# A two-layer diffusion step: first modulation by matrix products, HGRN level updates in one instruction, row broadcasts from two rounded parts

## The chip, the cores and the metric

The kernel runs on one core of one Trainium2 chip. The metric is the device time of one execution in microseconds (us). The kernel before takes 2850.07 us (median of three runs, 2849.15 to 2854.26). Everything below is told from one execution that the hardware profiler recorded. The engines are PE (TensorE, with its weight loads as PEld), DVE (VectorE), ACT (ScalarE), POOL (GpSimd) and SP (SyncE, which issues most DMAs).

## What is computed

One denoising step of a trunk with two layers, on 512 latent tokens and 128 prompt tokens of 1024 features, all in fp32. Cut to what matters here:

```python
def _modulation(cvec, w, b):                                  # once for c, once for c_ctx
    return (silu(cvec) @ w + b).reshape(cvec.shape[0], 9, D_MODEL)
def _ffn_sublayer(x, mod, j, g, b, w1, w3, w2):
    shift, scale, gate = _mod_parts(mod, j)
    h = x * (1 + scale) + shift
    y = (silu(h @ w1) * (h @ w3)) @ w2
    return _layernorm(ALPHA * x + 0.5 * gate * y, g, b)
for l in range(DEPTH):                # ffn, mixer, ffn; each with shift, scale, gate of its own
    ...
    # mixer of l = 0: windowed attention and a two-way mLSTM; l = 1: attention and a two-way HGRN2:
    #   S_t = diag(f_t) S_{t-1} + k_t v_t^T,  k_t = 1 - f_t,  o_t = S_t^T q_t
```

## The kernel before

Activations lie transposed: eight tiles of 128 features (`k`, KD = 8) by 640 tokens, handled in two halves of 384 and 256 tokens (HALVES; the prompt is the last 128). A product in nearly full precision is made of three products of rounded parts (`mm3`): the operand is split into a rounded part, copied by ACT (line 123), and the rest, subtracted by DVE (line 126). Weights come through four raw buffers (`rawp`, tag raw) and are split into `wp` (tile `w`) or `vp` (tile `wv`). The tokens `rawx` have buffers of their own.

A Python program writes the instructions in order and a scheduler puts each engine's queue in order, so every engine runs a fixed list. SP's list issues the loads, and a load whose buffer is still in use holds up all that stand behind it on SP.

`start` (lines 268 to 323) makes shift and scale of the first sublayer from two 1024x1024 blocks of `ada_w`. For each of eight column blocks `m` it loads two 1024x128 pieces (one DMA each), multiplies rows by silu(c) and adds them up on DVE (tile `acc`, lines 130 and 133), ACT (`acp`) and POOL (line 308), and lets PE add over the partitions by products with a vector of ones (`pm<-ones,acc`). After a block's shift and scale `mod`, `spread` makes the modulated tile `h` on ACT and splits it. The modulations of all later sublayers are a filler (`ada`, line 334, 128x512 steps on DVE), spread over the feed-forward layers.

`norm` (line 390) makes 1/sigma on POOL (`rs`), then broadcasts the rows rs and -mean*rs over the partitions by fp32 products with the identity (`prs`, `pnm`). The mLSTM of the even mixer broadcasts two rows for each head and direction in the same manner (`nmu`, line 1056, and `ab`, line 1073). They come from `ma`.

`hgrn_head` (line 1280) computes the decayed products of a head with a tree of seven levels. Tiles Q and K hold both directions (K = 1 - f, on POOL, line 1288). In levels 0 to 4, ACT gathers half of K of each direction into `kc` (two instructions), PE makes twenty 32x32 products (`lv`), and DVE puts the wanted ones into `diag` (line 1314). Then four updates of 128x320 elements multiply a half of each of Q and K by the level's totals, two on DVE and two on POOL (lines 1337 and 1338), and two small products make the totals of the next level (`hi<-hi`). Heads 0 and 1 run beside the projections of later heads (`weave`, temporaries `xarena` and `hw`), heads 2 and 3 with nothing but each other (`harena`).

Of the kernel before, what the change touches and what calls it, by code (L numbers as in the profile page):

```python
# [49 lines left out]
class Net:  # L50
# [146 lines left out]
    def setup(self):  # L197
# [30 lines left out]
        for row in rows:  # L228
            if row is None:
                pos = -(-pos // P) * P  # L230
                continue
# [11 lines left out]
    def vectors(self, b):  # L243
# [24 lines left out]
    def start(self, out):  # L268

        nc = self.nc  # L270
        w = self.i["ada_w"][0]
# [4 lines left out]
        sc = self.sc.rearrange("p (c k) -> p k c", c=2)
        most, dve = KD - 1, 1

        def finish(m, raw, acc):

            ps = self.pm()
            for part in range(2):
                o = ps[:, 2 * part:2 * part + 2]
                for k in range(most, KD):
                    self.mm(o, raw[:, part, k], sc[:, k], k == most, False)
                for n, t in enumerate(acc):
                    c = min(n, 1)
                    self.mm(o[:, c:c + 1], t[:, part * P:(part + 1) * P], self.ones, False, n == 2)
            for part in range(2):
                self.act(out[:, part, :, m], ps[:, 2 * part:2 * part + 2], AF.Identity, bias=b1[:, part, m:m + 1])  # L290
            a, b = HALVES[0]
            self.spread(0, m, self.x[:, m, a:b], out[:, 1], out[:, 0])
# [1198 lines left out]
```

## Time and profile before

| | |
|---|---|
| median of 3 runs | 2850.07 us |
| profiled execution, its own time | 2846.81 us |
| its span | 2845.0 us |
| PE busy | 2703.4 us, 95% |
| DVE busy | 1819.8 us, 64% |
| ACT, POOL busy | 961.4 us, 353.8 us |

The stages, by the timeline: first feed-forward layer to about 550 us, even mixer to 936, feed-forward to 1415, feed-forward of layer 1 to 1855, odd mixer to 2366 (HGRN heads from about 2140 to 2283), last feed-forward layer to the end. PE's busy time is modelled by the profiler, so 95% is no statement on its peak. Idle time of an engine counts only where the next stage waits for it.

### The profile page before, as it was taken

To read this page: it belongs to the slowest core of one execution; us is meant where nothing else is said; L and a number is where in the kernel's file an instruction comes from. 1 tells how busy PE (TensorE), PEld (TensorE's weight loads), DVE (VectorE), ACT (ScalarE), POOL (GpSimd) and SP (SyncE) were. 2 spreads that over 40 slices of the span, in tenths; PEclk is the share of its full clock that TensorE was granted. 3 is DMA by queue.
4 is the path that set the end of the run, shared out by engine and by line. 5 is a ranking of instruction groups with operands and counts; after the bars stand their busy time and mean duration, and the time that the engine had idled before them with its cause. 6 is when DMAs were issued, how large, how long until landed. Compare 5 with 4: busy or idle time off the path is not lost.

```text
span 2845.0 us, 47283 instructions
## 1 busy us (share of the span) xinstructions
PE 2703.4 (95%) x19221; PEld 2597.6 (91%) x19221; DVE 1819.8 (64%) x3573; ACT 961.4 (34%) x2009; POOL 353.8 (12%) x394
## 2 busy tenths in 40 slices
PE   6999999989998999999999999999998689999998
PEld 6999999988887999999899999988788589999997
DVE  8876765777657976533796773475677769333335
ACT  5411211555544421311432122155553435112122
POOL 4000000411003100000400000041104522000003
PEclk9999999999999999999999999999999799999999
DMA  7554543121222544422264452130111224223110
GB/s 197 177 149 126 168 122 102 61 63 39 63 69 70 151 146 126 126 67 75 60 181 132 124 165 82 45 97 20 42 42 51 75 71 132 71 73 97 60 53 38
DMA packets 321526, 270.56 MB, mean 95 GB/s; under 512 B 13834, under 2 KB 273692, under 8 KB 321308
## 3 DMA queue, kind: packets, MB, share of 16 engines
q1 hardware_dynamic: 320948, 267.39, 32.1%
q8 instruction: 151, 2.47, 0.4%
q14 instruction: 67, 0.55, 0.1%
q10 hardware_dynamic: 360, 0.14, 0.0%
HBM read 258.31 MB, written 9.18 MB: 94 GB/s over the span
## 4 chain that ended last, share of the span: by engine, by line
PE 73%; DVE 13%; DMA 5%; ACT 3%; issue 3%; POOL 2%; SPq 0%; DVEq 0%; ACTq 0%; POOLq 0%
PE ps L136 35%; PE po L136 21%; PE pj L136 5%; PE pn L136 3%; DVE acc L133 3%; DMA rawa<-in_ada_w 2%; DMA raw<-in_ffn_w 2%; PE pv L136 2%; DVE w L126 2%; PE pT L139 1%; PE s L136 1%; DVE wv L126 1%; DVE x L133 1%; DVE h L126 1%; DVE sum L126 1%
## 5 line engine op out<-in xcount | busy, mean ns | idle before, releaser
L136 PE MATMUL ps<-h,w 128*128 128x256 f32 (+1 forms) x7584 | 1122.9, 309 | 2.1 <-DVE h L126 1.8
L136 PEld LDWEIGHTS ps<-h,w 128*128 128x128 f32 x7584 | 1116.2, 190 | 3.5 <-DVE h L126 2.4
L136 PE MATMUL po<-g,wv 128*128 128x256 f32 (+1 forms) x4224 | 631.6, 310 | 6.7 <-DVE x L133 6.4
L136 PEld LDWEIGHTS po<-g,wv 128*128 128x128 f32 x4224 | 621.3, 188 | 14.1 <-DVE x L133 8.7
L133 DVE SCALAR_TENSOR_TENSOR x<-po,mod,x 128x128 f32<-128x128 f32 (+1 forms) x576 | 235.6, 435 | 277.2 <-PE po L136 275.8
L133 DVE SCALAR_TENSOR_TENSOR acc<-rawa,sc,acc 128x512 f32<-128x512 f32 (+1 forms) x496 | 351.2, 747 | 12.9 <-DMA rawa<-in_ada_w 11.5
L126 DVE TENSOR_TENSOR w<-raw,w 128x1024 fp32r<-128x1024 f32 x212 | 261.0, 1236 | 132.4 <-ACT w L123 131.8
L123 ACT ACTIVATE wv<-raw 128x1024 fp32r<-128x1024 f32 x116 | 120.1, 1055 | 568.3 <-PE po L136 451.4
L123 ACT ACTIVATE w<-raw 128x1024 fp32r<-128x1024 f32 x212 | 222.6, 1056 | 168.2 <-issue 76.7
L463 POOL TENSOR_TENSOR ssq<-ssq,sq 128x384 f32<-128x384 f32 (+1 forms) x84 | 84.1, 1001 | 1340.3 <-ACT sq L123 1318.8
L123 ACT ACTIVATE g<-gt 128x384 fp32r<-128x384 f32 (+1 forms) x176 | 82.1, 467 | 405.9 <-DVE gt L126 405.9
L126 DVE TENSOR_TENSOR wv<-raw,wv 128x1024 fp32r<-128x1024 f32 x116 | 143.0, 1239 | 95.4 <-ACT wv L123 95.1
L126 DVE TENSOR_TENSOR gt<-sl,ps 128x384 f32<-128x384 f32 (+1 forms) x176 | 85.4, 485 | 182.6 <-PE ps L136 177.6
L136 PE MATMUL pj<-h,w 128*128 128x256 f32 (+1 forms) x1056 | 185.2, 318 | 0.9 <-ACT w L123 0.8
L136 PEld LDWEIGHTS pj<-h,w 128*128 128x128 f32 x1056 | 161.4, 192 | 8.0 <-issue 3.4
L123 ACT ACTIVATE sl<-ps 128x384 f32<-128x384 f32 (+1 forms) x176 | 75.9, 433 | 224.9 <-PE ps L136 224.7
L136 PE MATMUL ps<-h,wv 128*128 128x256 f32 (+1 forms) x864 | 138.4, 312 | 2.9 <-ACT h L123 1.5
L136 PE MATMUL pn<-w,h 128*128 128x256 f32 x960 | 137.6, 289 | 0.0
L136 PEld LDWEIGHTS ps<-h,wv 128*128 128x128 f32 x864 | 127.5, 190 | 5.3 <-DVE h L126 2.1
L136 PEld LDWEIGHTS pn<-w,h 128*128 128x128 f32 x960 | 126.0, 193 | 1.2
L126 DVE TENSOR_TENSOR g<-gt,g 128x384 fp32r<-128x384 f32 (+1 forms) x176 | 85.7, 487 | 27.3 <-ACT g L123 27.3
L424 POOL TENSOR_SCALAR x<-x,agb 128x384 f32<-128x384 f32 (+1 forms) x80 | 74.0, 927 | 103.2 <-ACT h L123 71.9
(345 smaller groups left out, 2672.1 us busy)
## 6 DMA issues: line engine op xcount, KB each, us to landing
raw<-in_ffn_w SPq DMA_DIRECT2D x264, 512.0 KB, 3.9
rawa<-in_ada_w SPq DMA_DIRECT2D x144, 512.0 KB, 3.8
raw<-in_w_in_odd SPq DMA_DIRECT2D x18, 512.0 KB, 3.9
raw<-in_w_in_even SPq DMA_DIRECT2D x14, 512.0 KB, 4.0
raw<-in_w_in_even SPq DMA_DIRECT2D x16, 256.0 KB, 3.5
raw<-in_w_out_even SPq DMA_DIRECT2D x8, 512.0 KB, 4.6
raw<-in_w_in_odd SPq DMA_DIRECT2D x16, 256.0 KB, 3.3
raw<-in_w_out_odd SPq DMA_DIRECT2D x8, 512.0 KB, 4.5
```

The lines of the kernel that those rows point to most:

```text
L123: return self.nc.scalar.activation(out=out, in_=in_, func=func, **k)
L126: return self.nc.vector.tensor_tensor(out=out, in0=in0, in1=in1, op=op)
L133: return self.nc.vector.scalar_tensor_tensor(out=out, in0=in0, scalar=s, in1=in1, op0=op0, op1=op1)
L136: return self.nc.tensor.matmul(out=out, lhsT=lhsT, rhs=rhs, start=start, stop=stop)
L139: self.nc.tensor.transpose(out, in_, self.ident[:in_.shape[0], :in_.shape[0]])
L424: nc.gpsimd.tensor_scalar(out=x, in0=x, scalar1=agb[:, 0, k:k + 1], scalar2=agb[:, 1, k:k + 1], op0=ALU.mult, op1=ALU.add)
L463: nc.gpsimd.tensor_tensor(out=sums[1], in0=sums[1], in1=sq, op=ALU.add)
```

## The change

The first modulation: `ada_w` is loaded by rows, two contiguous 128x1024 pieces for each of eight `k`. PE multiplies them by silu(c), as a stationary operand of 32 columns of which two are used, in fp32, with four 512-column results in four column groups of the array. ACT and DVE copy the results to SBUF, and sixteen small products (`adat`) add up the groups and turn the rows into columns. Of the tokens, tile 0 is loaded before the last row block and the others after it. The weights of the first feed-forward block are asked for behind the first `h`.

The norms and the mLSTM broadcast rows that were split into two rounded parts (`spread_rows`: two products with a rounded identity in place of one fp32 product). The mLSTM's scratch moves from the pool `yp` to `fp`, with buffers of its own for the gate weights' staging.

The HGRN levels: K and Q of both directions lie in one tile of four planes, so one ACT instruction gathers `kc`, one DVE instruction of 1280 elements updates what a level changes, and one product makes the totals. 1 - f is made on ACT. The diff, cut to its core:

```diff
+    def spread_rows(self, out, cols):
+        for n, c in enumerate(cols):
+            self.mm(out, c.to_broadcast([P, out.shape[0]]), self.identr, n == 0, n == 1)
...
+        self.identr = c.tile([P, P], F32R, name="identr")
+        self.act(self.identr, self.ident)
...
+        z = self.ft(KD * 32, "scz").rearrange("p (k c) -> p k c", k=KD)
+        nc.gpsimd.memset(z, 0.0)
+        nc.vector.tensor_copy(out=z[:, :, 0:2], in_=self.sc.rearrange("p (c k) -> p k c", c=2))
...
-        late = None
-        for m in range(KD):
-            raw = self.vt((2, KD, P), F32, "rawa")
-            acc = [self.ft(2 * P, "acc") for _ in range(3)]
-            for part in range(2):
-                c0 = part * D + m * P
-                nc.sync.dma_start(out=raw[:, part], in_=w[:, c0:c0 + P].rearrange("(k p) c -> p k c", p=P))
-            av = [t.rearrange("p (a b) -> p a b", a=2) for t in acc]
-            for k in range(most):
-                self.ada_step(av[:2] if k < dve else av[:1], raw[:, :, k], k)
-            for k in range(dve, most):
-                t = av[2] if k == dve else self.ft(2 * P, "acp").rearrange("p (a b) -> p a b", a=2)
-                self.act(t, raw[:, :, k], scale=self.sc[:, 8 + k:9 + k])
-                if k > dve:
-                    nc.gpsimd.tensor_tensor(out=av[2], in0=av[2], in1=t, op=ALU.add)
-            if m == 0:
-                self.load_x(0)
-            if late is not None:
-                finish(*late)
-            late = m, raw, acc
-        finish(*late)
+        acc = [self.bank(t, "ada") for t in ("a1", "a2", "b", "b")]
...
+        for k in range(KD):
+            raw = self.vt((2048,), F32, "rawa")
+            for n in range(2):
+                c = slice(1024 * n, 1024 * n + 1024)
+                nc.sync.dma_start(out=raw[:, c], in_=w[k * P:(k + 1) * P, c])
+            if k == KD - 2:
+                self.load_x(0, (0,))
+            for q in range(4):
+                g = (k + q) % 4
+                self.mm(acc[q][32 * g:32 * g + 32], z[:, k], raw[:, 512 * q:512 * q + 512], k < 4, k >= 4)
+        rows = self.vt((4, 512), F32, "rows")
+        ps = self.pm("adat")
+        for q in (2, 0, 3, 1):
+            if q < 2:
+                nc.vector.tensor_copy(out=rows[:, q], in_=acc[q])
+            else:
+                self.act(rows[:, q], acc[q])
+        for q in (2, 0, 3, 1):
+            for m in range(4):
+                o = 2 * (4 * q + m)
+                self.mm(ps[:, o:o + 2], rows[:, q, m * P:(m + 1) * P], self.fold[:, 0:2])
+        pv = ps[:, 0:4 * KD].rearrange("p (a m c) -> p a c m", a=2, c=2)
+        for part in (1, 0):
+            self.tt(out[:, part], pv[:, part], b1[:, part, None, :].to_broadcast([P, 2, KD]), ALU.add)
+        self.load_x(0, (1, 2))
...
+                self.first = self.ffn_units(0, 0, 0, False)
         yield 1
-        self.load_x(1)
...
-        rs = self.sm(4, "rs")
+        rn = self.sm(8, "rn")
+        rs, nm = rn[:, 0:4], rn[:, 4:8]
         nc.gpsimd.tensor_tensor(out=rs[:, :nch], in0=var[:, :nch], in1=self.mhalf[:, :nch], op=ALU.pow)
-        nm = self.sm(4, "nmr")
         self.stt(nm[:, :nch], mean, -1.0, rs[:, :nch], ALU.mult, ALU.mult)
+        rn = rn.rearrange("p (a b) -> p a b", a=2)[:, :, :nch]
+        hl = self.small.tile([P, 2, 2, 4], F32R, tag="rnp", name="rnp")
+        hl = hl[:, 0, :, :nch], hl[:, 1, :, :nch]
+        self.split(*hl, rn)
         pr, pn = self.pm("prs"), self.pm("pnm")
-        for t, o in ((rs, pr), (nm, pn)):
+        for t, o in enumerate((pr, pn)):
             for c in range(nch):
-                self.mm(o[:, c * P:(c + 1) * P], t[:, c:c + 1].to_broadcast([P, P]), self.ident)
+                self.spread_rows(o[:, c * P:(c + 1) * P], [v[:, t, c:c + 1] for v in hl])
...
-        mc = Arena(self.yp.tile([P, self.YN], F32, tag="y", name="mc"))
+        mc = Arena(self.fp.tile([P, self.FN], F32, tag="f", name="mc"))
...
+        pair = self.pair("ma")
+        tmp = Arena(self.ft(384, "mtmp"))
...
+        self.act(pair[0], ma, scale=sgn)
+        self.stt(pair[1], ma, sgn, pair[0].bitcast(F32), ALU.mult, ALU.subtract)
...
-                self.mm(nmu[:, :b - a], nident[:, r:r + 1].to_broadcast([64, P]), ma[0:64, a:b])
+                for q in range(2):
+                    self.mm(nmu[:, :b - a], self.identr[0:64, r:r + 1].to_broadcast([64, P]), ma[q][0:64, a:b], q == 0, q == 1)
...
-                self.mm(ab[:, :b - a], self.ident[64:128, 64 + r:64 + r + 1].to_broadcast([64, P]), ma[64:128, a:b])
+                for q in range(2):
+                    self.mm(ab[:, :b - a], self.identr[64:128, 64 + r:64 + r + 1].to_broadcast([64, P]),
+                            ma[q][64:128, a:b], q == 0, q == 1)
...
-        Q, K = (t.rearrange("p (d t) -> p d t", d=2) for t in temps[0:2])
-        S, kcs = qT, temps[2:4]
-        for pl in (1, 0):
-            nc.gpsimd.tensor_scalar(out=K[:, pl], in0=ft[pl], scalar1=-1.0, scalar2=1.0, op0=ALU.mult, op1=ALU.add)
-            self.tt(Q[:, pl], qT, ft[pl], ALU.mult)
+        qk = temps[0].rearrange("p (d t) -> p d t", d=4)
+        base = qk[:, 0, 0:1]
+        Q, K = (qk[:, 1], qk[:, 2]), (qk[:, 3], qk[:, 0])
+        S, kcs = qT, temps[1:3]
+        ff = ft.rearrange("p d t -> p (d t)")
+        view = lambda t, off, *ap: bass.AP(tensor=t.tensor, offset=t.offset + off, ap=[t.ap[0]] + [list(a) for a in ap])
+        self.act(qk[:, 0::3], ft, AF.Identity, scale=-1.0, bias=1.0)
+        self.tt(view(base, 2 * NT, (-NT, 2), (1, NT)), ft, qT[:, None, :].to_broadcast([P, 2, NT]), ALU.mult)
...
-                self.act(halves(kc)[:, :, 0], halves(K[:, 1])[:, :, 0])
-                self.act(halves(kc)[:, :, 1], halves(K[:, 0])[:, :, 1])
-                qb = Q[:, 0, 0:1]
+                self.act(kc.rearrange("p (n two h) -> p n two h", two=2, h=hh),
+                         view(base, 0, (2 * hh, nb), (3 * NT + hh, 2), (1, hh)))
...
-            tot = [t.rearrange("p (n two) -> p n two", two=2) for t in tb]
-            br = lambda t: t[:, :, None].to_broadcast([P, nb, hh])
-            q0, k0, q1, k1 = halves(Q[:, 0]), halves(K[:, 0]), halves(Q[:, 1]), halves(K[:, 1])
-            self.tt(q1[:, :, 1], q1[:, :, 1], br(tot[1][:, :, 0]), ALU.mult)
-            self.tt(k1[:, :, 0], k1[:, :, 0], br(tot[1][:, :, 1]), ALU.mult)
-            nc.gpsimd.tensor_tensor(out=q0[:, :, 0], in0=q0[:, :, 0], in1=br(tot[0][:, :, 1]), op=ALU.mult)
-            nc.gpsimd.tensor_tensor(out=k0[:, :, 1], in0=k0[:, :, 1], in1=br(tot[0][:, :, 0]), op=ALU.mult)
-            tb = []
-            for d in range(2):
-                dst = ft[d][:, :nb]
-                self.tt(dst, tot[d][:, :, 0], tot[d][:, :, 1], ALU.mult)
-                tb.append(dst)
+            x = view(base, 0, (2 * hh, 2 * nb), (2 * NT + hh, 2), (1, hh))
+            one = ff[:, 0:1]
+            self.tt(x, x, view(one, 1, (2, 2 * nb), (-1, 2), (0, hh)), ALU.mult)
+            tot = ff[:, :4 * nb].rearrange("p (n two) -> p n two", two=2)
+            self.tt(ff[:, :2 * nb], tot[:, :, 0], tot[:, :, 1], ALU.mult)
```

Three places in the order of the instructions. The first is SP's list at the start of the program, before:

```order
L201 DMA ident<-in_c_ident 128x128
L300 DMA rawa<-in_ada_w 128x8x128 x2
L258 DMA rawx<-in_x_sample 128x1024 x3
L300 DMA rawa<-in_ada_w 128x8x128 x14
L163 DMA raw<-in_ffn_w 128x8x128 x4
L346 DMA rawa<-in_ada_w 128x2x512 x2
L163 DMA raw<-in_ffn_w 128x8x128 x2
L258 DMA rawx<-in_x_sample 128x1024
L258 DMA rawx<-in_x_prompt 128x1024
```

and now:

```order
L206 DMA ident<-in_c_ident 128x128
L299 DMA rawa<-in_ada_w 128x1024 x14
L271 DMA rawx<-in_x_sample 128x1024
L299 DMA rawa<-in_ada_w 128x1024 x2
L271 DMA rawx<-in_x_sample 128x1024 x2
L168 DMA raw<-in_ffn_w 128x8x128 x4
L356 DMA rawa<-in_ada_w 128x2x512 x2
L168 DMA raw<-in_ffn_w 128x8x128 x2
L168 DMA raw<-in_ffn_w 128x1024
L271 DMA rawx<-in_x_sample 128x1024
L271 DMA rawx<-in_x_prompt 128x1024
```

The loads of `ada_w` were sixteen column pieces behind three token tiles; now they are sixteen row pieces, with one token tile ahead of the last two and two behind. The second half's tokens stand behind one more weight load.

The second place is DVE's list in the HGRN levels of heads 2 and 3 (`harena` holds Q and K, `hi` the totals, `lv` and `diag` the 32x32 products), before:

```order
L126 TENSOR_TENSOR hi_20894<-hi_20894 128x160 x2
L1314 COPY_PREDICATED diag_22337<-lmask_21225,lv_22422 128x160
L126 TENSOR_TENSOR harena_22273<-harena_22273,hi_21357 128x160x2 x2
L126 TENSOR_TENSOR hi_20895<-hi_20895 128x160
L126 TENSOR_TENSOR hi_21357<-hi_21357 128x160
L1314 COPY_PREDICATED diag_22279<-lmask_21225,lv_22452 128x160
L126 TENSOR_TENSOR harena_22273<-harena_22273,hi_20894 128x80x4 x2
L126 TENSOR_TENSOR hi_20894<-hi_20894 128x80 x2
L1314 COPY_PREDICATED diag_22337<-lmask_21225,lv_22482 128x160
```

and now:

```order
L126 TENSOR_TENSOR harena_22057<-harena_22057,hi_20748 128x320x2x2
L1346 COPY_PREDICATED diag_22112<-lmask_21079,lv_22186 128x160
L126 TENSOR_TENSOR hi_20748<-hi_20748 128x320
L126 TENSOR_TENSOR harena_22057<-harena_22057,hi_20749 128x320x2x2
L1346 COPY_PREDICATED diag_22061<-lmask_21079,lv_22211 128x160
L126 TENSOR_TENSOR hi_20749<-hi_20749 128x320
```

For a level and head, two updates of 320 elements and two products of totals became one update of 1280 elements and one product. POOL's two updates have left its list.

The third is PE's list ahead of the even mixer (`po` is the last product of the feed-forward layer's second half, `wg` the gate weights of the mLSTM, `wv` those of a projection), before:

```order
L136 MATMUL pj_5286<-h_98,wg_5240 128x384 x6
L136 MATMUL pj_5398<-h_98,wv_5273 128x384 x3
L136 MATMUL po_5048<-g_4505,wv_4510 128x256
L136 MATMUL po_5069<-g_4505,wv_4510 128x256
L136 MATMUL pj_5398<-h_98,wv_5273 128x384 x3
L136 MATMUL pj_5286<-h_98,wg_5240 128x384
L136 MATMUL po_5048<-g_4505,wv_4510 128x256 x2
L136 MATMUL po_5048<-g_4506,wv_4515 128x256 x3
```

and now, in two pieces, first the start of `po`:

```order
L136 MATMUL po_4817<-g_4266,wv_4271 128x256
L136 MATMUL po_4838<-g_4266,wv_4271 128x256
L136 MATMUL po_4817<-g_4266,wv_4271 128x256 x2
L136 MATMUL po_4817<-g_4267,wv_4276 128x256 x3
L136 MATMUL po_4817<-g_4268,wv_4281 128x256 x3
```

then what follows the last `po`, at the second half's norm:

```order
L136 MATMUL prs_5000<-identr_107,rnp_4997 128x128 x4
L136 MATMUL pnm_5001<-identr_107,rnp_4997 128x128 x4
L136 MATMUL pj_5065<-h_98,wg_5017 128x384 x24
L136 MATMUL pj_5119<-h_98,wv_5047 128x384 x6
L136 MATMUL pj_5177<-h_98,wv_5052 128x384 x24
```

The products with `wg`, which stood between those of `po`, now stand behind the norm's broadcasts.

## Rows read from the trace of the kernel before

**Rows 1.** The page, busy time of each engine over the span.

```profile
PE 2703.4 (95%) x19221; PEld 2597.6 (91%) x19221; DVE 1819.8 (64%) x3573; ACT 961.4 (34%) x2009; POOL 353.8 (12%) x394
```

**Rows 2.** Windows: stage, busy us of each engine, granted clock, DMA share, GB/s.

```profile
0.00:85.00 85.00, 57.06 (x277) 52.89 (x278) 68.31 (x121) 45.72 (x111) 38.42 (x51) 1.00 0.72 194
85.00:545.00 460.00, 457.00 (x3128) 453.68 (x3127) 330.75 (x556) 121.90 (x191) 21.92 (x27) 1.00 0.44 131
...
760.00:860.00 100.00, 94.64 (x610) 79.56 (x609) 58.72 (x219) 45.73 (x157) 4.84 (x7) 1.00 0.25 63
...
2225.00:2280.00 55.00, 31.70 (x746) 27.05 (x745) 46.22 (x94) 18.92 (x47) 33.14 (x33) 0.72 0.09 30
```

**Rows 3.** Windows inside the start, same columns.

```profile
30.00:38.00 8.00, 5.01 (x24) 4.84 (x23) 7.86 (x12) 5.93 (x16) 6.87 (x9) 1.00 1.16 283
75.00:76.00 1.00, 0.51 (x5) 0.54 (x6) 0.00 (x0) 0.00 (x0) 0.00 (x0) 1.00 1.06 430
```

**Rows 4.** Groups of instructions, 0 to 85 us: count, busy, mean ns, idle before.

```profile
L308 POOL TENSOR_TENSOR acc<-acc,acp 128x256 f32<-128x256 f32 x40 | 32.9, 825 | 27.7 <-ACT acp L123 23.3 <-DVE acc L133 1.8
L133 DVE SCALAR_TENSOR_TENSOR acc<-rawa,sc,acc 128x256 f32<-128x256 f32 x48 | 32.8, 684 | 1.0
L136 PE MATMUL pm<-ones,acc 128*128 128x1 f32 x96 | 21.7, 340 | 11.8 <-DVE acc L133 8.5 <-POOL acc L308 3.3
...
L264 DVE COPY x<-pm 128x512 f32<-128x512 f32 x10 | 6.7, 685 | 3.8 <-PE pm L139 3.8
...
L123 ACT ACTIVATE h<-x,mod 128x384 f32<-128x384 f32 x8 | 5.6, 704 | 0.1
...
L123 ACT ACTIVATE w<-raw 128x1024 fp32r<-128x1024 f32 x4 | 4.2, 1055 | 0.0
L123 ACT ACTIVATE h<-h 128x384 fp32r<-128x384 f32 x8 | 4.1, 511 | 0.0
...
L123 ACT ACTIVATE mod<-pm,b 128x2 f32<-128x2 f32 x16 | 3.4, 260 | 23.0 <-PE pm L136 23.0
```

**Rows 5.** Timeline, 57 to 100 us: start, duration, engine, instructions, idle before.

```profile
64.53 9.98 PE L136 MATMUL ps<-h,w 128*128 128x384 f32 x56 [0.30 <-ACT h L123]
...
68.05 1.22 DVE L126 TENSOR_TENSOR w<-raw,w 128x1024 fp32r<-128x1024 f32 x1
...
69.75 0.57 SPq L258 DMA_DIRECT2D rawx<-in_x_sample  x1
...
75.49 1.06 PE L139 MATMUL pm<-ident,rawx 128*128 128x128 f32 x8 [0.98 <-DMA rawx<-in_x_sample]
...
84.32 15.91 PE L136 MATMUL ps<-h,w 128*128 128x256 f32 x109 [1.61 <-DVE h L126]
```

**Rows 6.** Groups of VectorE, 2224 to 2272 us: HGRN levels of heads 2 and 3.

```profile
L126 DVE TENSOR_TENSOR harena<-harena,hi 128x320 f32<-128x320 f32 x28 | 21.6, 801 | 0.0
...
L126 DVE TENSOR_TENSOR harena<-hi 128x640 f32<-128x640 f32 x4 | 3.3, 819 | 0.0
...
L126 DVE TENSOR_TENSOR hi<-hi 128x320 f32<-128x320 f32 x4 | 1.8, 484 | 0.9 <-POOL harena L1337 0.9
...
L126 DVE TENSOR_TENSOR hi<-hi 128x5 f32<-128x5 f32 x4 | 0.6, 157 | 0.6 <-POOL harena L1338 0.6
```

**Rows 7.** Tile harena, 2224 to 2285 us: min/median/max ns of one.

```profile
L126 DVE TENSOR_TENSOR harena<-harena,hi x28: 477/930/1329, 2232.4 to 2268.6; 128x320 f32<-128x320 f32 x28
```

**Rows 8.** Timeline, TensorE, one level's 32-column products.

```profile
2238.53 0.76 PE L136 MATMUL lv<-hi,harena 128*32 128x32 f32 x40 [4.95 <-DVE harena L126]
```

**Rows 9.** Groups of TensorE, whole span: row broadcasts of mLSTM.

```profile
L136 PE MATMUL ab<-mc,ident 64*128 64x384 f32 x16 | 7.3, 534 | 0.0
...
L136 PE MATMUL nmu<-mc 64*128 64x384 f32 x16 | 6.7, 519 | 0.6 <-DVE harena L133 0.6
```

**Rows 10.** Groups of TensorE, whole span: row broadcasts of the norms.

```profile
L136 PE MATMUL prs<-ident,rs 128*128 128x128 f32 x60 | 10.9, 319 | 8.8 <-POOL rs L410 8.8
```

**Rows 11.** Timeline, TensorE before the even mixer.

```profile
544.55 1.23 PE L136 MATMUL po<-g,wv 128*128 128x256 f32 x9
```

More of the change, by code (lines that the diff above doesn't have):

```diff
@@ L251, in v, with load_x @@
         return self.vec[:, a:a + n]
-    def load_x(self, hf):
+    def load_x(self, hf, tiles):
         nc = self.nc
-        for t in CHUNKS[hf]:
+        for t in tiles:
             src = self.i["x_sample"][0, t * P:(t + 1) * P] if t < 4 else self.i["x_prompt"][0]
@@ L275, in start @@
         self.ts(b1[:, 1], ab[:, 1], 1.0, ALU.add)
[L276 to L281, printed above, removed]
-            for part in range(2):
[L283 to L292, printed above, removed]
@@ L315, in start @@
+        for part in (1, 0):
+            self.tt(out[:, part], pv[:, part], b1[:, part, None, :].to_broadcast([P, 2, KD]), ALU.add)
+        self.load_x(0, (1, 2))
+        a, b = HALVES[0]
+        for k in range(KD):
+            self.spread(0, k, self.x[:, k, a:b], out[:, 1], out[:, 0])
+            if k == 0:
+                self.first = self.ffn_units(0, 0, 0, False)
         yield 1
-        self.load_x(1)
+        self.load_x(1, CHUNKS[1])
         a, b = HALVES[1]
@@ L935, in mlstm_rows @@
         rt = t[6]
-        ma = mc.take(NT)
+        ma = t[0]
         mu = ma[0:64]
@@ L1179, in odd @@
         q0 = [self.ft(e - a, "q") for a, e in HALVES]
-        room = [t[:, n] for t in (self.yt((2, NT), F32, "hi") for _ in range(2)) for n in range(2)] + [room5]
+        ya0, ya1 = (self.yt((2, NT), F32, "hi") for _ in range(2))
+        room = [ya1[:, 0], ya0, ya1[:, 1], room5]
         cols = self.hgrn_cols(room, 0, lb)
@@ L1198, in projections @@
         def projections(room, cols):
-            for h in range(4):
-                while len(room) < 5:
-                    t = self.vt((2048,), F32, "hi")
-                    room += [t[:, n * NT:(n + 1) * NT] for n in range(3)]
-                yield from self.hgrn_in(room[:5], cols or self.hgrn_cols(room, h, lb), w, h, heads)
-                room, cols = room[5:], None
+            yield from self.hgrn_in(room, cols, w, 0, heads)
+            left = []
+            for h in range(1, 4):
+                t = [self.vt((3, NT), F32, "hi") for _ in range(1 if len(left) == 2 else 2)]
+                if not left:
+                    room, left = [t[0][:, 2], t[0][:, 0:2], t[1][:, 0], t[1][:, 1]], [t[1][:, 2]]
+                elif len(left) == 1:
+                    room, left = [left[0], t[0][:, 0:2], t[0][:, 2], t[1][:, 0]], [t[1][:, 1:3], None]
+                else:
+                    room = [t[0][:, 0], left[0], t[0][:, 1], t[0][:, 2]]
+                yield from self.hgrn_in(room, self.hgrn_cols(room, h, lb), w, h, heads)
         proj = projections(room, cols[len(ahead):])
@@ L1220, in odd @@
         wr = [Arena(self.wp.tile([P, self.VN], F32, tag="w", name="hw")) for _ in range(2)]
[L1221 to L1222 removed]
+        self.weave(*both([[ar.take(4 * NT)] + [a.take(NT) for _ in range(2)] for a in wr], 0), (proj, 1))
         yd += self.pairs(yds[1][:, 1:2], (True,))
@@ L1225, in odd @@
         ar = Arena(self.hpool.tile([P, self.HN], F32, tag="h", name="harena"))
-        self.weave(*both([[ar.take(2 * NT) for _ in range(2)] + [ar.take(NT) for _ in range(2)] for _ in range(2)], 2))
+        self.weave(*both([[ar.take(4 * NT)] + [ar.take(NT) for _ in range(2)] for _ in range(2)], 2))
         self.out_group(wo, 1, yd, mod)
@@ L1266, in hgrn_in @@
     def hgrn_in(self, room, cols, w, h, heads):
-        qT, f0, f1 = room[0:3]
-        v, gt = (r.rearrange("p (c t) -> p c t", c=5) for r in room[3:5])
+        qT, f = room[0:2]
+        v, gt = (r.rearrange("p (c t) -> p c t", c=5) for r in room[2:4])
         for n, col in enumerate(cols):
@@ L1298, in hgrn_head @@
         self.act(D, ps)
-        tb = list(ft)
         for lev in range(7):
```

65 lines of the change are left out of this document (34 added, 31 removed).

## The prediction

> **What bounds the kernel now.** I read the page first: PE is busy for 95% of the span [rows 1], so an edit pays only where PE stands or where it takes products off PE. The windows by stage show where PE stands. In the first 85 us it is busy for 57.1 us, beside DVE at 68.3; from 85 to 545 it works 457.0 of 460 us, and DVE's 330.8 us there hide beneath it; in 760 to 860, the mLSTM, it works 94.6 of 100; in 2225 to 2280, the HGRN levels of heads 2 and 3, only 31.7 of 55 beside 46.2 of DVE, at a mean granted clock of 0.72 [rows 2]. The change touches three of these stages, and since PE is full from 85 to 545, a start that ends earlier moves everything behind it by as much.
>
> **The start.** Before, the modulation is paced by DVE and POOL, whose additions take 32.8 and 32.9 us, and by transfers at 283 GB/s [rows 3, 4]. What ends it is a chain: the last weight split of half 0 ends on DVE at 69.27 (68.05 plus 1.22), SP then gets to the second half's tokens at 69.75, PE transposes them at 75.49, and from 84.32 PE never stands again [rows 5]. I cost the new start by the moment at which those transposes can run, since all that follows them (copies, h, split) keeps its count.
>
> The new chain, step by step. (a) Transfers: eight row blocks of 1.05 MB and one token tile of 0.52 MB are 8.9 MB. Pieces of 512-byte packets moved at 283 GB/s, a microsecond with contiguous token and weight rows at 430 [rows 3]. At these two the last row block has left after 20.7 or 31.5 us; I take 390, short of the best microsecond, which gives 22.8, and add 3 us for the first issue and the landing: 26. (b) The last four products: 512 columns at a 32-column stationary. The nearest row is the 40 instructions (20 fp32 products of 32 columns in the four column groups) that took 0.76 us [rows 8], 0.15 us for four groups' worth of 32 columns; 16 times as many columns of four products give about 1 us if the groups run side by side, 4 us if not. I take 1.5. (c) Four copies of 512 columns on two engines, two each at 0.685: 1.4. (d) Sixteen fp32 products with a 128x128 weight, two instructions each: by the 96 that took 21.7 us [rows 4], 32 cost 7.2 us; I take 5, since those 96 partly stood between others' waits. Then two small additions, 0.5. The modulation is ready at 26 + 1.5 + 1.4 + 5 + 0.5 = 34.4 us. (e) The first h needs all three token tiles: the four copies left cost 4 x 0.685 = 2.7, with a transpose ahead of them: h starts at about 37.5. (f) ACT then makes eight h and their rounded parts, and four weight splits: 8 x (0.704 + 0.511) + 4 x 1.055 = 13.9 us [rows 4], and DVE's last subtraction 1.2: 52.6. (g) SP needs one more weight load ahead of the tokens, about 0.5, and from there 5.7 us as before (69.75 to 75.49): transposes at 58.8. The gain is 75.5 - 58.8, **16.7 us**; with a little for what collides in ACT's queue I take 16. At the bad ends of (a), (b) and (d) (31.5, 4, 7.2) the transposes run at about 72, and the gain is 4; at the best (20.7, 1, 3.5) it is 21. PE's work in half 0 (96 products of 384 columns at 9.98 us for 56, 17 us [rows 5]) ends by about 57, so it does not set the end. DVE has room in this stretch: its own 48 additions of 0.684 are gone [rows 4], and its list keeps the subtractions of h ahead.
>
> **The HGRN levels.** In heads 2 and 3 DVE is the chain. Per level and head it now runs two updates of 320 elements: 28 of them 21.6 us [rows 6], 477 ns at the least and 930 in the median [rows 7], because POOL runs its two beside them. The new update has 1280 elements. From 484 ns for 320 and 819 for 640 [rows 6] the slope is 0.335 us for 320, so 1280 cost 0.48 + 3 x 0.335 = 1.49 us, and 14 cost 20.9. Its bounds are 1.34 us (four times the slope, no fixed part) and 3.7 (four at the 930 of today). The small products of totals go from four to two per level of two heads: today's seven groups, from 1.8 us at 320 elements down to 0.6 at 5 [rows 6], sum to 9.6 us, and half as many of twice the size cost about 4.7. Q goes from 4 x 0.82 to 2 x 1.49. DVE's sum falls by 0.7 + 4.9 + 0.3 = 5.9 us, and nothing is late in its place, since PE and ACT are idle for a third to a half of this stage [rows 2]. The same edits in heads 0 and 1 run beside projections; I count a fifth of it there, 1.2. POOL's 1 - f moves to ACT, which is busy for 18.9 of 55 us there [rows 2]. Together **-7 us**; from -13, if POOL's late finishes are also on the chain, to +16 at 2.6 us an update.
>
> One rule weighs against the new update. At level 0 it jumps between two planes after every element, and at level 1 after every second. In rows, an update that takes every second element (level 0 today) is no slower than the least of 477 ns [rows 7]. The Trainium skill, "SBUF — State Buffer", section "Specifications (TRN2)", says that SBUF has 16-byte lines and wants at least two hits on a line for full bandwidth; by it the level-0 update has one hit a line. No row here shows a jump at every element. By the rule, with twice the time for level 0, the sum would be 6 us worse (the fourth rival below has the working).
>
> **The mLSTM broadcasts.** Each fp32 product is two instructions: `ab` with 384 columns takes 7.3 us for 16, so 0.91 for a product, `nmu` 6.7, so 0.84 [rows 9]. Two rounded products take 2 x 0.178 by the 9.98 us for 56. Eight of each save 4.4 and 3.9 us; the 256- and 128-column ones save about two thirds as much again, some 11 to 13 in all. They overlap with loads, and PE waits for DVE there for 5 of 100 us, so I take 40%: **-5 us**, between 0 and -11. The split of `ma` (about 0.75 us each on ACT and DVE) lies beside projections on PE.
>
> **The norms.** After rs, the new chain has the product on DVE that was beside it, an ACT copy and a DVE subtraction: 0.26 for ACT's 128x2 [rows 4] and 0.16 for DVE's smallest [rows 6], twice, so about 0.65 us, and it saves about 0.3 on PE. Before, PE's wait for rs sums to 8.8 us [rows 10] over twelve norms, so most of them hide it. If four show it in full, that is 2.6; I take **+2.5**, from 0 to +6, where ACT has a weight split of 1.06 us ahead of the copy.
>
> **The gate weights.** Before, products with `wg` fill PE between groups of nine `po`, which took 1.23 us [rows 11] while DVE's two updates of x, a sum and an h took about as long or longer. Without them PE waits there, and the same products come later, behind the norm, where they may cover its wait: **+2**, from -1 to +5.
>
> **Sum.** -16 - 7 - 5 + 2.5 + 2 = -23.5 us on the profiled execution's 2846.8 (span 2845.0 and 1.8 around it), giving 2823.3; the median of the runs stands 3.3 above that execution, so 2826.6, and I forecast **2827 us**.
>
> **Rivals.** First, the start gives back most: transfers stay at 283 GB/s because something other than the packet size holds them, and the four column groups take turns. That is 8.5 us more in (a) and 2.5 in (b), a gain of 5 in place of 16: 2838 us. Against it stand the 430 and the 0.76 [rows 3, 8]; for it, that neither was read on these loads and these shapes. Second, the HGRN stage gains nothing: updates cost 1.9 (four of 477, no fixed part saved), 0.4 x 14 = 5.7 us, or PE's products, at a granted clock of 0.72 in the mean, become the bound: 2834 us. Third, on the other side, the update's jumps between planes cost DVE on every level what POOL's presence costs it today, 3.7 us: 2.2 more for each of 28, in full for the 14 of heads 2 and 3 and half for the others, 46 us against the sum's 23.5: 2873 us. It makes the kernel no faster from 1.49 + 23.5/21 = 2.6 us an update. Against it: updates with a step are no slower than others today [rows 7]. Fourth, only the level-0 update, with a jump after each element, takes twice as long: four of 1.5 more, 2833 us. That is what the rule of the Trainium skill above would do.
>
> **Chances.** The forecast (2814 to 2832) 0.56, the first rival 0.15, the second 0.10, the fourth 0.06, several of these at once (2840 to 2850) 0.06, the third 0.04, more gain than forecast 0.03. The measurement tells about 0.2%, 5.7 us, from no change: faster takes all but the third and most of the several at once, 0.91; the same 0.05; slower 0.04. The range reaches from 2808 (start 20, HGRN 12, mLSTM 10) to 2842, and leaves out the third and most of the several.
>
> **What will show it.** PE's transposes of the second half near 59 us; the last `ada` products near 27 us and `adat` at some 5 us; in the HGRN stage 1280-element updates near 1.49 us, DVE no longer full, and the stage some 6 to 8 us shorter; `nmu` in pairs near 0.36 us; prs waits longer by about half a microsecond each. An update above 2.6 us, or second-half transposes after 70 us, would make the forecast wrong.

## The result and the profile after

The changed kernel takes 2826.86 us (median of four runs, 2822.27 to 2827.78), the kernel before 2851.19 beside it: 0.9911 of it, with an interval of 0.9893 to 0.9928. Timed once more beside other kernels it took 2823.16, 0.9916 (0.9902 to 0.9930). The forecast was 2827. Its profiled execution has a span of 2825.2 us and 1.8 around it, against 2845.0. The engines' busy line of the page answers to [rows 1]:

```profile
PE 2707.6 (96%) x19189; PEld 2590.9 (92%) x19189; DVE 1774.7 (63%) x3466; ACT 946.8 (34%) x1946; POOL 252.6 (9%) x293
```

PE does as much as before; DVE and POOL do 45 and 101 us less. The windows of the stages, as in [rows 2], with the stretches moved by about what the stage moved:

```profile
0.00:70.00 70.00, 52.35 (x258) 36.57 (x258) 31.77 (x57) 27.18 (x54) 6.92 (x13) 0.88 0.72 243
...
70.00:530.00 460.00, 454.26 (x3094) 450.80 (x3095) 327.86 (x555) 119.92 (x185) 20.32 (x21) 0.99 0.44 129
...
745.00:845.00 100.00, 94.87 (x600) 83.71 (x599) 57.67 (x211) 45.89 (x147) 4.78 (x6) 0.90 0.25 66
...
2210.00:2260.00 50.00, 34.74 (x760) 29.00 (x761) 40.60 (x65) 18.07 (x36) 1.60 (x1) 0.73 0.11 32
```

The first stage is over at 70 in place of 85 us, with DVE at 31.8 busy us in place of 68.3. In the HGRN stage POOL's 33 us are gone. The first row's clock of 0.88 is 17 us at 1.2 GHz from 30.2 on, 1.3 us into the small products `adat`; they cover the rest of `adat` and the token transposes behind it. The third row has the surprise: the mLSTM's granted clock is 0.90 in the mean, where it was 1.00.

To see where the time went I take one mark at each stage, POOL's 1/sigma of a norm, before and after (start, duration; 128x3 is half 0, 128x2 half 1). Before:

```profile
514.76 0.87 POOL L410 TENSOR_TENSOR rs<-var,mhalf 128x3 f32<-128x3 f32 x1 [1.76 <-DVE var L130]
...
550.56 0.72 POOL L410 TENSOR_TENSOR rs<-var,mhalf 128x2 f32<-128x2 f32 x1 [1.53 <-DVE var L130]
...
907.75 0.86 POOL L410 TENSOR_TENSOR rs<-var,mhalf 128x3 f32<-128x3 f32 x1 [2.02 <-DVE var L130]
...
1890.63 0.69 POOL L410 TENSOR_TENSOR rs<-var,mhalf 128x2 f32<-128x2 f32 x1
...
2338.21 0.86 POOL L410 TENSOR_TENSOR rs<-var,mhalf 128x3 f32<-128x3 f32 x1 [3.51 <-DVE var L130]
```

After:

```profile
498.68 0.87 POOL L421 TENSOR_TENSOR rn<-var,mhalf 128x3 f32<-128x3 f32 x1 [1.76 <-DVE var L130]
...
535.80 0.72 POOL L421 TENSOR_TENSOR rn<-var,mhalf 128x2 f32<-128x2 f32 x1 [1.53 <-DVE var L130]
...
899.79 0.86 POOL L421 TENSOR_TENSOR rn<-var,mhalf 128x3 f32<-128x3 f32 x1 [2.02 <-DVE var L130]
...
1878.49 0.69 POOL L421 TENSOR_TENSOR rn<-var,mhalf 128x2 f32<-128x2 f32 x1
...
2316.33 0.86 POOL L421 TENSOR_TENSOR rn<-var,mhalf 128x3 f32<-128x3 f32 x1 [4.10 <-DVE var L130]
```

The differences are 16.1 us at the end of the first feed-forward layer's half 0, 14.8 at its half 1, only 8.0 in the even mixer, 12.1 ahead of the odd mixer and 21.9 in it. So the start gives some 15 us, the even mixer gives 7 of them back, and the odd mixer adds 10. The forecast's sum was met by terms of other sizes.

The start follows the forecast's chain step by step (timeline of the changed kernel, as [rows 5]):

```profile
13.22 6.01 PE L136 MATMUL ada<-rawa,scz 128*32 128x512 f32 x28
...
27.14 1.05 PE L136 MATMUL ada<-rawa,scz 128*32 128x512 f32 x4 [0.23 <-DMA rawa<-in_ada_w]
...
28.87 5.81 PE L136 MATMUL adat<-fold,rows 128*128 128x2 f32 x32 [0.68 <-ACT rows L123]
...
38.30 0.71 ACT L123 ACTIVATE h<-x,mod 128x384 f32<-128x384 f32 x1 [8.99 <-DVE x L277]
...
50.01 2.35 DVE L126 TENSOR_TENSOR w<-raw,w 128x1024 fp32r<-128x1024 f32 x2
...
52.78 0.43 SPq L271 DMA_DIRECT2D rawx<-in_x_sample  x1
...
59.67 1.07 PE L139 MATMUL pm<-ident,rawx 128*128 128x128 f32 x8
...
70.22 19.97 PE L136 MATMUL ps<-h,w 128*128 128x256 f32 x128 [0.24 <-DVE h L126]
```

The last piece of the last row block is in at 27.1 (26 forecast). Its two products, four instructions, take 1.05 us; the forecast had 1.5 for the four of a whole block, whose first two ran while the last piece was still on its way. Then `adat` takes 5.81 (5), the first h begins at 38.3 (37.5), the weight splits of half 0 end at 52.4 (52.6) and the second half's tokens are transposed at 59.67 (58.8). The loads of the start, from 10 to 26 us, moved 412 GB/s (window, last column):

```profile
10.00:26.00 16.00, 13.88 (x66) 3.47 (x68) 0.91 (x3) 0.31 (x2) 0.00 (x0) 1.00 1.02 412
```

In the HGRN levels the update of 1280 elements takes what the slope gave, except at level 0 (timeline of DVE, then its groups in 2205 to 2250 us):

```profile
2221.47 2.58 DVE L126 TENSOR_TENSOR harena<-harena,hi 128x1280 f32<-128x1280 f32 x1
...
2224.84 1.48 DVE L126 TENSOR_TENSOR harena<-harena,hi 128x1280 f32<-128x1280 f32 x1
...
2226.87 1.48 DVE L126 TENSOR_TENSOR harena<-harena,hi 128x1280 f32<-128x1280 f32 x1
```

```profile
L126 DVE TENSOR_TENSOR harena<-harena,hi 128x1280 f32<-128x1280 f32 x14 | 22.8, 1641 | 1.0 <-PE full L136 1.0
...
L126 DVE TENSOR_TENSOR hi<-hi 128x640 f32<-128x640 f32 x2 | 1.6, 810 | 0.0
```

The level-0 update of a head takes 2.58 us, every other 1.48. That is the forecast's fourth rival. It was a loss inside a larger gain. From the first 32x32 product of heads 0 and 1 to the last of heads 2 and 3, the levels 0 to 4 of all four heads with what lies between the pairs took 106.5 us before (first and last start of each group stand behind its times):

```profile
L136 PE MATMUL lv<-hi,xarena x40: 196/196/217, 2152.3 to 2152.7; 128*32 128x32 f32 x40
...
L136 PE MATMUL lv<-harena x400: 205/241/264, 2232.2 to 2258.8; 128*32 128x32 f32 x134
```

and take 94.6 now:

```profile
L136 PE MATMUL lv<-hi,hw x80: 196/196/217, 2142.7 to 2144.8; 128*32 128x32 f32 x80
...
L136 PE MATMUL lv<-harena x400: 210/241/263, 2212.4 to 2237.3; 128*32 128x32 f32 x134
```

### The profile page after: what moved, and what is told of

Its sections match the earlier page's. It is cut to its first block, busy times and chain, and to the rows that moved or that the text cites. A ratio compares the mean times of both kernels' runs of the same rounds, so it can differ in the third digit from the quotient of the medians.

```text
span 2825.2 us, 46791 instructions
## 1 busy us (share of the span) xinstructions
PE 2707.6 (96%) x19189; PEld 2590.9 (92%) x19189; DVE 1774.7 (63%) x3466; ACT 946.8 (34%) x1946; POOL 252.6 (9%) x293
## 5 line engine op out<-in xcount | busy, mean ns | idle before, releaser
L133 DVE SCALAR_TENSOR_TENSOR acc<-rawa,sc,acc 128x512 f32<-128x512 f32 x448 | 319.6, 757 | 11.1 <-DMA rawa<-in_ada_w 10.6
L136 PE MATMUL pj<-h,wv 128*128 128x384 f32 (+1 forms) x480 | 84.8, 326 | 2.0 <-DVE t L126 1.4
```

Of the source, the lines that this page charges most:

```text
L133: return self.nc.vector.scalar_tensor_tensor(out=out, in0=in0, scalar=s, in1=in1, op0=op0, op1=op1)
L136: return self.nc.tensor.matmul(out=out, lhsT=lhsT, rhs=rhs, start=start, stop=stop)
```

## The experiments

All ratios are to the kernel before on the same chip, with 95% intervals. Two or three microseconds between two kernels are not told apart by time alone, so I read the marks too. For every profile I took the same stretches:

| kernel | half 1's 1/sigma to first `pv` | mLSTM heads 0, 1 | heads 2, 3 | of that at half clock | odd mixer |
|---|---|---|---|---|---|
| before | 69.1 | 45.9 | 50.3 | 0 | 447.6 |
| changed | 74.5 | 42.9 | 56.0 | 20.5 | 437.8 |
| changed, again | 74.9 | 42.9 | 52.4 | 13.7 | 436.0 |
| start alone | 70.2 | 45.8 | 49.1 | 0 | 449.9 |
| HGRN alone | 69.2 | 45.9 | 50.0 | 0 | 436.7 |
| mLSTM in fp32 | 73.9 | 45.9 | 50.4 | 0 | 434.3 |
| gate weights early | 70.4 | 42.9 | 51.7 | 10.2 | 439.2 |
| level 0 in two | 74.4 | 42.9 | 50.5 | 10.2 | 431.4 |
| norms in fp32 | 74.5 | 42.8 | 50.9 | 10.2 | 434.7 |
| tokens early | 74.4 | 42.9 | 50.7 | 10.2 | 439.8 |
| last three together | 70.7 | 42.9 | 52.2 | 13.7 | 431.5 |
| broadcasts twice | 74.5 | 47.4 | 49.0 | 0 | 437.4 |
| start and HGRN | 69.0 | 45.9 | 49.1 | 0 | 436.1 |
| same, level 0 in two, tokens early | 70.3 | 45.9 | 49.3 | 0 | 432.8 |

(us; `pv` is attention's product of probabilities and values; mLSTM heads 0 and 1 count from the first `kq` to the last start of `num`, heads 2 and 3 from there to the last start of `dC`; "last three together" is gate weights early, level 0 in two and tokens early; the odd mixer runs from half 1's 1/sigma ahead of it to half 0's behind it; the half clock is the time granted at 1.2 GHz, from the profile's clock record.)

**The start alone**: the new `start` and `load_x` in the kernel before.

> The kernel before with the new start alone (modulation by products, row loads, order of token loads). Theory A: the whole gain of the start, 15 us by the anchors of the two traces (the first norm's 1/sigma of half 0 at 514.8 before, 498.7 after), stays to the end, since the loss that the changed kernel shows in the even mixer (its 1/sigma of half 0 stands only 8.0 us earlier) comes from other edits: 15 us less than before, 0.9947 of it. Rival B: the even mixer cannot use an earlier start (its weights and the filler come no earlier), so the loss belongs to the start: 8 us less, 0.997, and the 1/sigma of the even mixer's half 0 at about 900 rather than 893.

2834.87 against 2853.27, 0.9935 (0.9923 to 0.9947): theory A. Its even mixer's 1/sigma stands at 892.7, 15.1 us ahead of before. Rival B falls.

**The HGRN levels alone**: the new `odd` and `hgrn_*` in the kernel before.

> The kernel before with the new HGRN levels alone. Theory A: the odd mixer is shorter by 8 us (9.7 by the anchors of the two traces, of which some is noise), 0.997 of before; level-0 updates take 2.58 us and all others 1.48. Rival B: most of the odd mixer's 9.7 us came from the norms or from a TensorE clock that happened to be higher: under 4 us less, 0.9985 or more.

2841.55 against 2853.27, 0.9959 (0.9946 to 0.9973): 12 us, and 11 in the table's odd mixer. The table's odd mixer scatters by 5 us between traces with the same HGRN levels; the stretch from the first to the last 32x32 product does not: 106.4 and 106.5 us in the two traces with the old levels, 94.5 to 94.6 in the nine with the new. So 12 us, theory A with more than it expected. What each edit within the levels adds (POOL's updates gone, one gather, one product of totals) was not separated.

**Both together**, the rest as before.

> The kernel before with the start and the HGRN levels alone, the norms, the mLSTM and the gate weights as before. Theory A: the two gains add up (0.9935 and 0.9959 alone, 18 and 12 us): 0.9895, 2821, below the changed kernel's, since what that adds on top is worth less than the 4 us that its gate weights cost. Rival B: they share cover and give 24 together, 2826.

2818.63 against 2846.87, 0.9899 (0.9883 to 0.9915). The gains add up. The changed kernel was 0.9916 beside it, so the rest of the change is worth nothing or less; the intervals overlap.

**The gate weights early**:

```diff
-        tmp = Arena(self.ft(384, "mtmp"))
+        tmp = Arena(self.yt((384,), F32, "mtmp"))
```

> The changed kernel with the gate weights staged in a buffer of the pool yp, as before, so that their 24 products stand among the last products of the feed-forward layer again and not behind the norm. Theory A: this order cost 4 to 5 us (24 x 0.178 us of products that were free before; the first attention product stands 9.4 us earlier than before where the norm ahead stands 14.8 earlier): 4 us less than the changed kernel, 0.9897 of before, first attention product near 606. Rival B: the chain of the gates on ACT and DVE behind these products sets what follows, or the filling only moves the wait: under 1.5 us.

2819.19 against 2853.27, 0.9874 (0.9856 to 0.9892), about 10 us under the changed kernel's 0.9911, of which the stretch in question explains 4.1 (74.5 to 70.4). Another 4.3 lie in the mLSTM's heads 2 and 3 (56.0 to 51.7), by the time at half clock, which differs from trace to trace; what is left lies within the two intervals. PE's rows show the 4.1. In the changed kernel, `po` waits, and the 24 products come after the norm:

```profile
525.44 1.29 PE L136 MATMUL po<-g,wv 128*128 128x256 f32 x9
527.99 2.63 PE L136 MATMUL po<-g,wv 128*128 128x256 f32 x18 [1.26 <-DVE x L133]
...
538.05 4.38 PE L136 MATMUL pj<-h,wg 128*128 128x384 f32 x24
```

with the staging in yp they stand between the `po` again (start of the run, and two pieces between `po`):

```profile
515.35 1.21 PE L136 MATMUL pj<-h,wg 128*128 128x384 f32 x6
...
525.34 1.04 PE L136 MATMUL pj<-h,wg 128*128 128x384 f32 x5
...
529.30 1.75 PE L136 MATMUL pj<-h,wg 128*128 128x384 f32 x9
```

The first `pv` stands at 610.3 and at 604.7 us. Theory A.

**The mLSTM's broadcasts in fp32 again**, cut:

```diff
-                for q in range(2):
-                    self.mm(nmu[:, :b - a], self.identr[0:64, r:r + 1].to_broadcast([64, P]), ma[q][0:64, a:b], q == 0, q == 1)
+                self.mm(nmu[:, :b - a], ma[1][:, r:r + 1].to_broadcast([64, P]), ma[0][0:64, a:b])
```

> The changed kernel with the mLSTM's row broadcasts as single fp32 products again. Theory A: these broadcasts are worth about nothing (they gain 3 us in heads 0 and 1 and lose it in heads 2 and 3, where TensorE was granted half its clock for 20 us in place of 3): within 3 us of the changed kernel, about 0.991 of before, with heads 2 and 3 at the full clock and heads 0 and 1 some 3 us longer. Rival B: they are worth the 5 us forecast, hidden by another loss: 5 us more than the changed kernel, 0.993. Rival C: they cost what the even mixer lost: 5 us less, 0.9895.

The split of `ma` goes with them. 2822.4 against 2853.27, 0.9895 (0.9882 to 0.9909): rival C's figure, with an interval that reaches theory A's, so the time does not decide. The table is clearer: heads 0 and 1 lose the 3.0 us that the rounded products gave, to the tenth in all kernels; heads 2 and 3 get back the full clock (which the kernel before has there throughout: 0 us at half clock, not 3).

**The broadcasts twice**:

```diff
-                for q in range(2):
+                for q in (0, 1, 0, 1):
```

> The changed kernel with every row broadcast of the mLSTM made twice (four rounded products in place of two, the first two overwritten): PE gets as many broadcast columns as the fp32 products had passes. Theory A: the half clock in heads 2 and 3 (10 to 20 us in six traces with the rounded broadcasts, none there in four with fp32) came from PE's lighter load: with the products doubled heads 2 and 3 keep the full clock and take 50 us (56.0 in the changed kernel's trace), heads 0 and 1 go from 42.9 back to about 46. Rival B: it is the kind of product or chance: half clock remains and both pairs get longer, 3 us more in all.

2821.64 against 2846.87, 0.9908 (0.9894 to 0.9921), by time not told from the changed kernel. Windows in heads 2 and 3 (PE, PEld, DVE, ACT, POOL, granted clock), changed kernel, fp32, and rounded twice:

```profile
819.00:829.00 10.00, 9.24 (x32) 6.29 (x31) 7.37 (x29) 3.42 (x11) 0.00 (x0) 0.65 0.17 54
829.00:839.00 10.00, 10.00 (x56) 9.83 (x55) 4.24 (x19) 3.46 (x15) 0.00 (x0) 0.66 0.00 1
```

```profile
812.00:822.00 10.00, 9.51 (x49) 6.31 (x47) 7.75 (x26) 5.26 (x15) 0.00 (x0) 1.00 0.33 98
822.00:832.00 10.00, 9.35 (x49) 6.58 (x49) 7.89 (x29) 2.08 (x7) 0.00 (x0) 1.00 0.25 67
```

```profile
813.00:823.00 10.00, 9.55 (x64) 8.05 (x63) 8.73 (x33) 4.64 (x13) 0.00 (x0) 1.00 0.39 126
823.00:833.00 10.00, 9.99 (x66) 8.71 (x64) 7.45 (x29) 2.94 (x12) 0.00 (x0) 1.00 0.24 68
```

In the changed kernel a mean of 0.65 says that PE had 1.2 in place of 2.4 GHz for about 7 of the 10 us; it finished 32 instructions in the first window. With fp32, and with twice the rounded products, it stays at 1.00. What PE did just before the long fall (at 822.1 in the changed kernel), and at the same place in the other two, in the same order:

```profile
815.30:822.10 6.80, 6.04 (x31) 4.27 (x31) 6.61 (x27) 2.48 (x7) 0.00 (x0) 1.00 0.01 0
...
814.70:821.40 6.70, 6.23 (x32) 4.22 (x28) 5.26 (x19) 2.56 (x7) 0.00 (x0) 1.00 0.13 36
...
815.80:822.50 6.70, 6.41 (x39) 5.47 (x39) 6.20 (x25) 2.40 (x6) 0.00 (x0) 1.00 0.22 69
```

PE was busy for 6.04 of 6.80 us ahead of the fall, and for 6.23 and 6.41 of 6.70 where the clock stayed. Theory A: the lighter broadcasts cost the clock, and the clock takes back most of what they save. It rests on one trace with the broadcasts twice, whose heads 0 to 3 took 96.4 us together, 1.4 more than the 95.0 of the single ones in the mean. Over seven traces with single rounded broadcasts, heads 2 and 3 took 50.5 to 56.0 us, mean 52.1; over six with fp32 49.1 to 50.4, mean 49.7.

**The level 0 in two instructions**:

```diff
-            self.tt(x, x, view(one, 1, (2, 2 * nb), (-1, 2), (0, hh)), ALU.mult)
+            if lev == 0:
+                for j in range(2):
+                    x = view(base, j * (2 * NT + 1), (2, 2 * nb))
+                    self.tt(x, x, view(one, 1 - j, (2, 2 * nb)), ALU.mult)
+            else:
+                self.tt(x, x, view(one, 1, (2, 2 * nb), (-1, 2), (0, hh)), ALU.mult)
```

> The changed kernel with the level-0 update of the HGRN tree in two instructions of 640 elements, each within two planes at every second element, so that nothing jumps between planes after each element. Theory A: the jumps cost 1.1 us in each of the four level-0 updates (2.58 against 1.48 us for the other levels); two instructions cost 2 x 0.82 = 1.64, DVE saves 0.94 a head, and the two of heads 2 and 3 are on the path: 2 us less than the changed kernel, 0.9905 of before, level-0 instructions near 0.82. Rival B: level 0 is slow because its operand of totals is the widest, not because of the jumps: two instructions of 1.3 us each, no difference.

2814.24 against 2850.55, 0.9877 (0.9862 to 0.9892). DVE's timeline:

```profile
2211.30 1.55 DVE L126 TENSOR_TENSOR harena<-harena,hi 128x640 f32<-128x640 f32 x2
...
2213.74 1.48 DVE L126 TENSOR_TENSOR harena<-harena,hi 128x1280 f32<-128x1280 f32 x1
```

Two instructions over the same elements and totals take 1.55 us together: rival B falls. What the split took away is the jump after each element of Q and K, and with it the totals' order in swapped pairs (second before first); the two are not separated. The odd mixer is 431.4 to 432.8 us in the three traces with this edit and 434.3 to 439.8 in the nine with one instruction, 5 us less in the mean but with a scatter as large. The stretch from the first to the last 32x32 product is steady: 91.3 to 91.4 in place of 94.5 to 94.6, 3.2 us, of which 1.0 in heads 0 and 1 and 2.2 in heads 2 and 3. So all four heads count, not two, and theory A's 2 us was short by the first pair's part.

**The norms in fp32 again**, the two lines of `split` and `spread_rows` undone.

> The changed kernel with the norms' row broadcasts as single fp32 products again. Theory A, as forecast: each norm that is not covered is shorter by about 0.5 us, 2.5 us less in all, 0.9902 of before. Rival B, from the anchors (the 36 us between the two halves' 1/sigma of the first norm are the same with and without): nothing, within 1 us.

2819.99 against 2850.55, 0.9893 (0.9879 to 0.9908). The interval overlaps the changed kernel's, and by the marks the norm behind the odd mixer and the layer after it, together, take 460.7 us in the changed kernel, 458.0 here and 459.6 before. Over all traces that stretch is 459.4 to 460.7 with rounded norms (eight, mean 460.0) and 458.0 to 459.6 with fp32 ones (six, mean 459.1), 0.9 us; between the two halves' 1/sigma behind layer 0's second feed-forward layer the rounded ones are the shorter, 39.5 against 40.6 in the mean. (The 36 us of rival B are 35.8 before and 37.1 in the changed kernel.) A cost of the norms is not told from nothing: this speaks for rival B, and doesn't show it.

**The second half's tokens early**: their loads issued behind the first two weight loads.

> The changed kernel with the loads of the second half's tokens issued right behind the first two weight loads and not behind the fifth and sixth and the first w2 row. Theory A: after the change, what ends the start is the same chain as before it (weight split, then SP, then token loads, 59.7 us for the transposes); with the tokens in SBUF by about 37 us the second half's h follow the first half's on ACT without a stop, and PE's idle time between 54 and 70 us goes: about 8 us less than the changed kernel, 0.988 of before, and the steady run of 256-column products from about 61. Rival B: ACT and DVE set the pace there and the extra 1 MB delays the first weights: within 2 us.

2816.44 against 2850.55, 0.988 (0.9865 to 0.9895), 9 us under the changed kernel's 0.9911. By the marks the start gains less: the first 1/sigma stands at 496.1 here and at 494.6 and 492.7 in the two runs below that have this edit, and at 496.9 to 499.5 in the nine others with the new start. That is 4 us in the mean, between the two theories, although the tokens are transposed 15.6 us earlier. The tokens are transposed from 44.0, and then DVE's list, with filler steps (`acc`) between the subtractions of h, keeps PE waiting:

```profile
44.04 1.48 PE L139 MATMUL pm<-ident,rawx 128*128 128x128 f32 x6
...
60.75 1.20 DVE L133 SCALAR_TENSOR_TENSOR acc<-rawa,sc,acc 128x512 f32<-128x512 f32 x1
...
61.87 0.94 DVE L126 TENSOR_TENSOR h<-h 128x256 fp32r<-128x256 f32 x1
...
65.84 0.62 PE L136 MATMUL ps<-h,w 128*128 128x256 f32 x3 [0.37 <-DVE h L126]
```

**Those three together.**

> The changed kernel with the three edits together: gate weights staged in yp, level 0 in two instructions, second half's tokens loaded early. If the three are independent: 7.7 (measured for the first) + 2 + 8 = 18 us less than the changed kernel, about 2809, 0.985 of before. If the earlier start is lost again in the even mixer, 10 us less, 2817.

2808.27 against 2850.55, 0.9854 (0.9838 to 0.9871): the best version, 16 us under the changed kernel by the ratios, whose intervals do not touch.

**Start, HGRN, level 0 in two and early tokens**, broadcasts in fp32 (and, with them, the mLSTM's scratch in the pool `yp` as before).

> The same with level 0 in two instructions and the second half's tokens loaded early, so it differs from the combined version (0.9854) only in the row broadcasts of the norms and the mLSTM, in fp32 here. Theory A: those broadcasts are worth nothing together: 0.9854 within 0.0012. Rival B: they are worth 3 us or more, 0.9866. Rival C: they cost, 0.984.

2813.45 against 2846.87, 0.9886 (0.9870 to 0.9901). Against 0.9854 this speaks for rival B, on another chip; by the two spans, 2809.8 and 2806.0, it is 4 us. The table gives the mLSTM no part in it beyond 0.1 us. The marks spread it: this run is 1.9 us ahead at the first norm, loses 2 us between the halves' 1/sigma behind layer 0's second feed-forward layer (41.6 against 39.5) and the rest in parts of less than 2 us. The cause stays open.

**The changed kernel again.**

> The changed kernel once more, beside the others on one chip, since six variants came out below its first 0.9911 (0.9893 to 0.9928). Theory A: its first timing was at its upper end and it stands near 0.9900 (2822), so that putting back the norms' or the mLSTM's fp32 broadcasts changes nothing. Rival B: it stands at 0.9911 again (2826), and each of those two edits costs it 4 to 5 us. In its trace the even mixer from the first attention product to its 1/sigma takes 284 to 290 us, by how long TensorE is at its half clock in the mLSTM's heads 2 and 3.

0.9916, 2823.16: rival B by the ratio, theory A by the time, for the kernel before was faster on that chip too. So single edits of 4 us are settled here by the marks, not by the times.

## Why the prediction was right, term by term

- **The start, -16**: shown, 18 us by time alone and 16 by the marks. Each step came within a microsecond or so. The early tokens show how far the chain holds: with the tokens, its last link, 15.6 us earlier the first norm came some 4 us earlier only; what keeps PE waiting then is DVE's list, in the rows of that run. The first rival (283 GB/s, column groups in turn) fell. The loads moved 412 GB/s from 10 to 26 us, above the 390 of the forecast. Of the products, the 28 instructions from 13.22 on, fourteen products, took 6.01 us, 0.43 each; in turn they would take 1 us each by the rival's figure.
- **HGRN, -7**: the mechanism was right, the size short; alone it gives 12 (8 to 15). DVE's sum in heads 2 and 3 fell by 4.6 rather than 5.9 (with 0.7 that the forecast did not count, the sum of both K), since two level-0 updates took 1.1 longer each, and that pair is some 4.5 us shorter. The mis-sized part is what I gave heads 0 and 1, a fifth of that: of the 12.0 us, 5.2 lie between their first 32x32 product and the last instruction on their tiles (59.6 to 54.4) and 2.2 between the pairs. DVE was on their path too, beside the projections: of the 2.1 us that the level-0 split saves it there, 1.0 comes off the stretch. That all 5.2 are DVE's is not shown. The fourth rival's case came true within this term, 1.1 in place of 1.5 us a head. The rule of the Trainium skill, "SBUF — State Buffer", section "Specifications (TRN2)", that a line wants two hits, agrees with both rows: one element a jump costs 2.58, two elements a jump 1.48. It gives no price; twice the time was the forecast's assumption.
- **mLSTM, -5**: failed in size. PE's saving came, 3.0 us in heads 0 and 1, and heads 2 and 3 gave back 2.4 in the mean through the clock: about -0.6. The step that failed is taking the price of a product at today's clock.
- **Norms, +2.5**: not seen. Some 0.9 us in the one stretch that shows a loss, and as much gained in another; the extra steps are there (ahead of the even mixer prs starts 1.22 us after the start of 1/sigma, before 0.78), but that four norms show them in full was wrong.
- **Gate weights, +2**: the sign was right, the size 4 to 5. The 24 products cost their full 24 x 0.18 us behind the norm, and hid no wait there.

With 18, 12 and 0.6 gained, 4.4 lost to the gate weights and up to 1 to the norms, the terms give 25 to 26 us; the ratios give 24 and 25. The forecast's hit on 2827 is thus partly luck: HGRN was 5 too small, the start and the norms each some 2 too cautious, and mLSTM and the gate weights together 7 too good. The third rival (2.6 us an update) was met by one level in seven.

## What to carry to other kernels

Cost a moved start by its chain to the last transfer that everything waits for, not by the work removed; here each step came within about a microsecond. Then ask which chain ends next. Products that stand between waiting ones are free only there; look where a change of buffers puts them. When two access patterns are folded into one instruction, look how many neighbouring elements it takes before it jumps.

## What the runs showed of the hardware

- DVE, 1280 fp32 elements: 1.48 us with two or more neighbours before a jump between planes, 2.58 with one; as two instructions at every second element 1.55 together (the totals, the second operand, then come in order).
- Fewer broadcast products in the mLSTM's heads 2 and 3 left PE at half clock for 10 to 20 us in seven traces of seven; with fp32 products (six traces) or the rounded ones twice (one) it kept the full clock there. Heads 2 and 3 took 52.1 us in the mean with the fewer products, 49.7 with fp32 and 49.0 with the rounded ones twice.
